# Joining the small product stages of an interleaved decoder block into common bursts, with a fourth weight buffer

## The chip, the core and the metric

The kernel runs on one core of a Trainium2 chip. The metric is the device time of one execution in microseconds (us); lower is better. A core has a matrix engine (TensorE, PE in the profile, with its weight loads shown as PEld), three engines for elementwise work (VectorE is DVE, ScalarE is ACT, GpSimd is POOL), and queues that issue DMA transfers (SP's is the one used for weights here).

## The reference

One decoder block on 256 tokens plus 16 meta tokens, all in float32 with a model width of 2048:

```
xn = rms(h)
z_rwkv, z_fox, z_gate = split(xn @ w_in)
y_a = rwkv7(token_shift(z_rwkv))          # 16 heads of 64: a linear recurrence over the tokens
y_b = fox(z_fox)                          # 16 heads of 64: causal attention with a forget gate
g_a, g_b = split(sigmoid(z_gate))
h = h + (g_a * (y_a @ w_a) + g_b * (y_b @ w_b)) @ w_o
gate, up = split(rms(h) @ w_gate_up)
out = h + (silu(gate) * up) @ w_down      # the 16 meta rows are dropped
```

The weights are 274 MB in all and are read once. Each float32 product is made of products of a high and a low part ("hl" in names), so that the matrix engine runs at its full rate.

## The kernel before

**The stream.** All weight products form one long stream of jobs on the matrix engine. A job takes one weight tile: `wload` (lines 301 to 325) issues the DMA into a `raw` tile (512 KB), ACT makes its high part `wh` (line 322) and DVE its low part `wl` (line 323). `raw` has `RAWB` buffers, `wh` and `wl` have `WB` buffers each, 3 of each here. `run` loads one job ahead of the one that multiplies. The order of instructions on the matrix engine is written out by hand (`manual_schedule`); the order on ACT, DVE, POOL and SP is made by the framework's scheduler, except for the first jobs.

**The order of the jobs.** First the `lora` jobs, then for each of four head groups g the projections k, v, r (272, 272 and 258 columns), a small job for decay and gate (`rwkv_w2` and so on), the FoX projections q, k, v (256, 272, 272 columns), and two gate jobs (256 columns). After the fourth group nine more gate jobs follow, then one more, then the branches, `w_o`, gate and up, and `w_down`.

**The small products.** Between the stream's matrix products stand the small ones of RWKV and FoX. Each of these chains is a Python generator that yields the planner's distance in ns until its next stage. `streams` holds the generators with their due times; `clock[0]` is the planner's clock, which counts only the stream's products. `slot` (line 360) is called after each triple of stream products (3n/2.4 ns of planner time for n columns). If a stage is due, the one with the earliest due time is emitted: its matrix products go into PE's order at this place, its other work to the other engines. After that, no stage comes for `GAP`, or for `MIX` times the stage's estimated matrix time `clock[2]`. I call the run of small matrix products of one stage a burst. The stages of one group with matrix products, in order:

- RWKV: `ss` and `kx` (norms of k), `mat` three times (the chunk matrices), `bs` (bonus), `trbk` twice, `trv`, `tr` (transposes); then a triangular solve on DVE with DMAs through DRAM (lines 829 to 849) and the wait `LANE`; then the chain: `rhs` of the meta tokens, `QT` with `u`, `X` with `s`, and four times `rhs`, `u` with `y`, `s` with `y`; last `yT`.
- FoX: `fss` twice and `fx` (norms), `pvm` with `pv` (transposes of v), and for each of two head pairs `sc` (scores, then softmax on DVE and ACT), `ppt` with `ptm` (transposes of the probabilities, copied to `pT` and `pM` by ACT), and `po` (the output).

These are 36 bursts a group, 144 in all, and one more of the forget gate. `psa` has four PSUM banks for them (`aux_ps`), the stream's own are in `psm`.

Of the kernel before, what the change touches and what calls it, by code (L numbers as in the profile page):

```python
# [12 lines left out]
AF = mybir.ActivationFunctionType  # L13
# [5 lines left out]
P = 128  # L19
D = 2048  # L20
NMETA = 16

T = 256
L = NMETA + T
# [23 lines left out]

RAWB = 3
WB = 3  # L50
ZB = 6
# [11 lines left out]
LANE = 24000  # L63
GAP = 250
LERP = 2800
BIAS = 7000
STEP = 1000
NORM = 4200
SUMS = 2000
X_RS = 1400  # L70
X_SPREAD = 1400
X_V = 1900
X_SC = 1600
X_EXP = 1100
X_DIV = 2600
X_PT = 1400
Y_SQ = 1400
# [6 lines left out]
Y_BONUS = 1200  # L84
Y_TRBK = 1400
Y_TRV = 1100
Y_TR0 = 1600
Y_RHS = 1400
Y_U = 1400
Y_XT = 1400  # L90
Y_QT = 1200
Y_GN = 1400
# [5 lines left out]
def hybrid_block(ctx, tc, A, out, dbg=None):  # L98
# [244 lines left out]

    def spawn(gen, delay):
        streams.append([clock[0] + delay, gen])

    def stage(st):
        try:
            st[0] = clock[0] + (next(st[1]) or HOP)
        except StopIteration:  # L350
            streams.remove(st)

    def pe_mm(out_, lhsT, rhs, start, stop, skip=False):
# [7 lines left out]
    def slot(ns):  # L361


        clock[0] += ns
        if clock[0] < clock[1]:
            return
        due = [st for st in streams if st[0] <= clock[0]]
        if due:
            clock[2] = 0.0
            stage(min(due, key=lambda st: st[0]))  # L370
            clock[1] = clock[0] + max(GAP, MIX * clock[2])

# [297 lines left out]
    def rwkv_bg(g, box):  # L670
# [15 lines left out]
        nc.scalar.activation(sq, kk, AF.Square)  # L686
        yield Y_SQ
        kn_ = rw.tile([P, 12], F32, tag="kn", name=f"kn{g}", bufs=2)
# [4 lines left out]
        backs = [spread(kr_, m, L, f"kx{g}{m}") for m in range(2)]  # L693
        yield Y_SPREAD
        for m in range(2):
# [37 lines left out]
        split(*parts, sq[:, :, :T])  # L733
        yield Y_AB

# [3 lines left out]
        for m in range(2):  # L739
            pss = [aux_ps(f"mat{g}{m}{h}") for h in range(2)]  # L740
            for c in range(4):
                for h in range(2):
                    pe_mm(pss[h][:, c * P:(c + 1) * P], bk[hb(h), m, c].rearrange("p x t -> p (x t)"),
                                     ar[hb(h), :, m, tok(c)], start=True, stop=True)
            for h in range(2):
                nc.vector.tensor_tensor(NK[:, h, 4 * m:4 * m + 4, :], pss[h].rearrange("p (c w) -> p c w", w=P),
                                        bcast(mup, 4), op=ALU.mult)
            yield Y_MAT
        pss = [aux_ps(f"mat0{g}{h}") for h in range(2)]
# [28 lines left out]
        for h in range(2):  # L778
            for m in range(2):
                nc.gpsimd.tensor_copy(NK[0:HD, h, 4 * m:4 * m + 4, 0:HD],  # L780
                                      ar[hb(h), 0, m, NMETA:].rearrange("p (c t) -> p c t", t=HD))
        yield Y_NEXT

        bo = ot(f"bo{g}")
        for m in range(2):
# [5 lines left out]
            nc.gpsimd.tensor_scalar(bo[:, m, :], bo[:, m, :], vi("gn_b", m), None, op0=ALU.add)  # L791
        yield Y_BONUS

# [5 lines left out]
        for m in range(2):  # L799
            ps = aux_ps(f"trbk{g}{m}")  # L800
            for c in range(4):
                pe_tr(ps[:, c * P:(c + 1) * P], bkf[:, 4 * m + c, :], ident)
            nc.scalar.activation(BK[:, :, 4 * m:4 * m + 4, :].rearrange("p h c d -> p c h d"),
                                 ps.rearrange("p (c h d) -> p c h d", h=2, d=HD), AF.Copy)
            yield Y_TRBK
        ps = aux_ps(f"trv{g}")
# [4 lines left out]
        for cc in range(2):  # L811
            nc.scalar.activation(SV[HD:, :, cc::2, :].rearrange("p h i d -> p i h d"),
                                 ps[hb(cc), :].rearrange("p (i h d) -> p i h d", h=2, d=HD), AF.Copy)
        yield Y_TRV
        ps = aux_ps(f"tr0{g}")
# [29 lines left out]
        for h in range(2):  # L845
            for q in range(2):
                nc.sync.dma_start(X[h * HD + 32 * q:h * HD + 32 * q + 32, :, 32 * q:32 * q + 32], d2v[h, q, :32])
            nc.sync.dma_start(X0[h * HD:h * HD + 16, :, 0:32], d3.rearrange("(h m) r t -> h r m t", h=2)[h])
        yield LANE

# [3 lines left out]
        def step(c, S, BK, SV, NK, X, Y):  # L854
# [11 lines left out]
            nc.scalar.activation(R, pv2(ps), AF.Copy)  # L866
            yield Y_RHS
            ps = aux_ps(f"u{g}{c}")
# [10 lines left out]
            for h in range(2):  # L879
                nc.vector.tensor_copy(SV[0:nt, h, mine, :], pv2(ps)[h * HD:h * HD + nt])  # L880
            yield Y_U
            if not last:
# [20 lines left out]
            if not first:  # L903
                nc.scalar.activation(Y.rearrange("p (m c) v -> p m c v", m=2)[:, :, c, :], pv2(psy), AF.Copy)
            yield HOP

# [7 lines left out]
        next(meta_steps)  # L914
        yield Y_XT
        ps = aux_ps(f"QT{g}")
# [6 lines left out]
        next(meta_steps)  # L923
        yield Y_QT
        ps = aux_ps(f"X12{g}")
# [22 lines left out]
        nc.vector.tensor_tensor(Y, Y, s2.unsqueeze(2).to_broadcast([P, 8, HD]), op=ALU.mult)  # L948
        yield NORM
        ps = aux_ps(f"yT{g}")  # L950
# [28 lines left out]
    def fox_jobs(g):  # L979
# [18 lines left out]
        def norms():  # L998
            while len(done) < 2:
                yield  # L1000
            yield from rsqrt_steps(fx, hr, hs, [P, 20], "ht")
            yield X_RS

            nc.vector.tensor_tensor(hs[:, 0:8], hs[:, 0:8], hr[:, 0:8], op=ALU.mult)
            backs = [spread(hr[:, 8:20], m, L, f"fx{g}{m}") for m in range(2)]
            yield X_SPREAD
            for m in range(2):
                nc.vector.tensor_tensor(kn[:, m, :], kn[:, m, :], backs[m](), op=ALU.mult)
            yield
            ready.append(1)  # L1010

        def post(dst, n):
            def f(pss):
                sqs = []
                for m in range(2):
                    ps = pss[m]
                    if dst is vv:
                        nc.scalar.activation(dst[:, m, :], ps[:, :n], AF.Copy)
                        continue
                    sq = fx.tile([P, L], F32, tag="sqf", name=f"sqf{g}", bufs=3)  # L1020
                    if dst is qn:
                        halves(dst[:, m, :], ps)
                        nc.scalar.activation(sq[:, :n], dst[:, m, :], AF.Square)
                    else:
                        nc.scalar.activation(sq[:, :n], ps[:, :n], AF.Square)
                        nc.scalar.activation(dst[:, m, :], ps[:, :n], AF.Copy, scale=qk8)
                    sqs.append(sq)
                if dst is vv:
                    spawn(fox_bg(g, qn, kn, vv, hs, hr, ready), HOP)
                else:  # L1030
                    spawn(sums(sqs, dst, n), SUMS)
                    if dst is kn:
                        spawn(norms(), PREP)
            return f
# [4 lines left out]
    def fox_bg(g, qn, kn, vv, hs, hr, ready):  # L1039
# [18 lines left out]
        cmb = cmask.unsqueeze(1).to_broadcast([P, 2, P])  # L1058
        for m in range(2):

# [9 lines left out]
            nc.gpsimd.tensor_tensor(bias[:, :, d1], bias[:, :, d1], cmb, op=ALU.add)  # L1070
            yield BIAS
            sums = fx.tile([P, 4], F32, tag="sums", name=f"sums{g}{m}", bufs=2)

            nq = [NMETA + P, L]
            cq_ = [slice(0, nq[0]), slice(nq[0], nq[0] + nq[1])]
# [5 lines left out]
            for t in range(2):  # L1081
                n = nq[t]
                for h in range(2):
# [7 lines left out]
                    nc.scalar.activation(s[:, :n], s[:, :n], AF.Exp, scale=r, bias=nm,  # L1091
                                         accum_out=sums[:, 2 * t + h:2 * t + h + 1])
            yield X_SC + X_EXP
            nc.vector.reciprocal(sums, sums)
            for t in range(2):
                for h in range(2):
                    s = sc_t[h, t][:, :nq[t]]
                    nc.vector.tensor_scalar(s, s, sums[:, 2 * t + h:2 * t + h + 1], None, op0=ALU.mult)
            yield X_DIV


            ptm = aux_ps(f"ptm{g}{m}")
            pts = []
            for h in range(2):
                ppt = aux_ps(f"ppt{g}{m}{h}")
                for c, t, k in ((T - 96, 0, 1), (0, 0, 0), (P, 1, 0), (T + 32, 1, 1)):
                    pe_tr(ppt[:, c:c + P], sc_t[h, t][:, k * P:(k + 1) * P], ident)
                pe_tr(ptm[:NMETA, h * P:(h + 1) * P], sc_t[h, 1][:, 2 * P:L], ident)
                pT = fx.tile([P, 416], F32, tag="pT", name=f"pT{g}{m}{h}", bufs=2)
                nc.scalar.activation(pT, ppt[:, :416], AF.Copy)  # L1110
                pts.append(pT)
            nc.scalar.activation(pM[:NMETA], ptm[:NMETA, :2 * P].rearrange("p (h q) -> p h q", h=2)[:, :, 96:], AF.Copy)
            yield X_PT
            po = aux_ps(f"po{g}{m}")
            for i in range(3):
                for h in range(2):
                    vs = slice(m * P + h * HD, m * P + (h + 1) * HD)
                    o = po[hb(h), :T]
                    if i == 0:
                        pe_mm(o, vt[:, 0, vs], pts[h][:, 0:T], start=True, stop=False)  # L1120
                    elif i == 1:
                        pe_mm(o[:, 96:], vt[:, 1, vs], pts[h][:, T:], start=False, stop=False)
                    else:
                        pe_mm(o[:, T - 32:], vm[:, vs], pM[:, h, :], start=False, stop=True)
            nc.scalar.activation(yb[:, 2 * g + m, :], po[:, :T], AF.Copy)
            yield

# [263 lines left out]
```

## Time and profile before

| what | value |
|---|---|
| median of three runs | 1565.6 us (1564.53, 1565.60, 1565.76) |
| the profiled execution: its own time, its span | 1564.75 us, 1563.0 us |
| busy: PE, PEld, DVE, ACT, POOL | 1553.5, 1366.3, 1015.7, 766.8, 104.3 us |
| granted TensorE clock, mean | 1.000 |
| read from HBM | 274.43 MB, 180 GB/s over the span |

The span runs from the first to the last instruction; the execution's own time has 1.75 us around it. Ends of matrix products are modelled, so what a burst costs is read from starts: how far apart two products of the stream stand with the burst between them, less what they are apart without one.

### The profile page before, as it was taken

What the parts mean: (1) busy time and instruction counts of PE and PEld (TensorE: products, weight loads), DVE (VectorE), ACT (ScalarE), POOL (GpSimd) and SP (SyncE); (2) the same over time, 40 slices, a digit from 0 to 9 for tenths busy, and PEclk for the clock granted to TensorE, in tenths of its full rate; (3) what the DMA queues carried; (4) which work ended last, traced back from release to release, by engine and by line L of the source; (5) the groups of instructions that cost most, each with busy time, mean ns of one, the idle gap of its engine ahead of it and who ended that gap; (6) DMA issues with size and microseconds to landing.
All of it is one profiled execution on the core that took longest, in us unless ns stands there. A gap on an engine that the chain in (4) does not pass through costs nothing.

```text
span 1563.0 us, 26173 instructions
## 1 busy us (share of the span) xinstructions
PE 1553.5 (99%) x10225; PEld 1366.3 (87%) x10225; DVE 1015.7 (65%) x1854; ACT 766.8 (49%) x1118; POOL 104.3 (7%) x194
## 2 busy tenths in 40 slices
PE   9999999999999999999999999999999999999998
PEld 9999988989889888999888888888888888888887
DVE  7878688677768856875655666566566656444443
ACT  6655455465445544654445554454445544333332
POOL 2121103102203100000000000000000000000000
PEclk9999999999999999999999999999999999999999
DMA  7556546546545566777666666666666666666664
GB/s 243 173 154 173 158 126 179 157 119 168 166 135 148 161 182 192 248 225 227 189 182 179 188 186 190 188 188 189 188 189 189 185 193 187 188 202 199 187 200 131
DMA packets 211483, 283.33 MB, mean 181 GB/s; under 512 B 23888, under 2 KB 128352, under 8 KB 211360
## 3 DMA queue, kind: packets, MB, share of 16 engines
q1 hardware_dynamic: 206752, 277.53, 60.8%
q10 hardware_dynamic: 4608, 4.13, 0.8%
q8 instruction: 80, 1.31, 0.4%
q14 instruction: 43, 0.35, 0.1%
HBM read 274.43 MB, written 7.19 MB: 180 GB/s over the span
## 4 chain that ended last, share of the span: by engine, by line
PE 94%; DVE 3%; DMA 1%; ACT 1%; issue 1%; SPq 0%; POOL 0%; DVEq 0%; ACTq 0%
PE up L392 10%; PE gt L392 10%; PE zg L392 7%; PE dn L1255 5%; PE dn L1253 5%; PE dn L1254 5%; PE up L394 5%; PE gt L394 5%; PE zg L394 3%; PE f L333 2%; PE f L392 2%; PE f L335 2%; PE f L334 2%; PE br L334 2%; PE br L335 2%; PE br L333 2%
## 5 line engine op out<-in xcount | busy, mean ns | idle before, releaser
L323 DVE TENSOR_TENSOR wl<-raw,wh 128x1024 fp32r<-128x1024 f32 (+1 forms) x496 | 605.3, 1221 | 439.7 <-ACT wh L322 437.8
L322 ACT ACTIVATE wh<-raw 128x1024 fp32r<-128x1024 f32 (+1 forms) x496 | 521.2, 1052 | 624.5 <-PE dn L1254 144.4
L392 PE MATMUL gt<-hts,wh 128*128 128x512 f32 x704 | 245.0, 394 | 0.0
L392 PE MATMUL up<-hts,wh 128*128 128x512 f32 x704 | 244.9, 394 | 0.0
L394 PE MATMUL gt<-hts,wl 128*128 128x256 f32 x660 | 186.2, 282 | 0.0
L394 PE MATMUL up<-hts,wl 128*128 128x256 f32 x660 | 186.0, 282 | 0.0
L392 PE MATMUL zg<-xhl,wh 128*128 128x512 f32 x512 | 184.3, 403 | 0.0
L392 PEld LDWEIGHTS up<-hts,wh 128*128 128x128 f32 x704 | 130.1, 188 | 26.4
L392 PEld LDWEIGHTS gt<-hts,wh 128*128 128x128 f32 x704 | 130.1, 188 | 26.3
L1254 PE MATMUL dn<-wh,acl 128*128 128x512 f32 x352 | 139.5, 396 | 0.0
L1253 PE MATMUL dn<-wh,ach 128*128 128x512 f32 x352 | 139.5, 396 | 0.0
L1255 PE MATMUL dn<-wl,ach 128*128 128x512 f32 x352 | 139.5, 396 | 0.0
L394 PE MATMUL zg<-xhl,wl 128*128 128x256 f32 x480 | 135.0, 281 | 0.0
L394 PEld LDWEIGHTS up<-hts,wl 128*128 128x128 f32 x660 | 124.7, 189 | 1.8
L394 PEld LDWEIGHTS gt<-hts,wl 128*128 128x128 f32 x660 | 124.7, 189 | 1.8
L392 PEld LDWEIGHTS zg<-xhl,wh 128*128 128x128 f32 x512 | 94.5, 188 | 20.8 <-issue 1.8
L394 PEld LDWEIGHTS zg<-xhl,wl 128*128 128x128 f32 x480 | 90.6, 189 | 1.1
L1255 PEld LDWEIGHTS dn<-wl,ach 128*128 128x128 f32 x352 | 66.3, 188 | 16.2
L1254 PEld LDWEIGHTS dn<-wh,acl 128*128 128x128 f32 x352 | 66.3, 188 | 16.2
L1253 PEld LDWEIGHTS dn<-wh,ach 128*128 128x128 f32 x352 | 66.3, 188 | 16.1
L333 PE MATMUL f<-xhl,wh 128*128 128x272 f32 x256 | 77.7, 303 | 0.0
L335 PE MATMUL f<-xhl,wl 128*128 128x272 f32 x256 | 73.8, 288 | 0.0
(459 smaller groups left out, 2777.6 us busy)
## 6 DMA issues: line engine op xcount, KB each, us to landing
raw<-in_w_gate_up_dram SPq DMA_DIRECT2D x176, 512.0 KB, 3.6
raw<-in_w_in_dram SPq DMA_DIRECT2D x160, 512.0 KB, 4.2
raw<-in_w_down_dram SPq DMA_DIRECT2D x88, 512.0 KB, 4.7
raw<-in_w_o_dram SPq DMA_DIRECT2D x32, 512.0 KB, 4.6
raw<-in_w_branch_a_dram SPq DMA_DIRECT2D x16, 512.0 KB, 3.9
raw<-in_w_branch_b_dram SPq DMA_DIRECT2D x16, 512.0 KB, 3.8
zgd<-zg ACTq DMA_DIRECT2D x30, 128.0 KB, 2.4
gate<-zgd SPq DMA_DIRECT2D x15, 256.0 KB, 5.8
```

The source lines that it names most:

```text
L322: nc.scalar.activation(wh[:prow, cs_], raw[:prow, cs_], AF.Copy)
L323: nc.vector.tensor_tensor(wl[:prow, cs_], raw[:prow, cs_], wh[:prow, cs_].bitcast(F32), op=ALU.subtract)
L333: nc.tensor.matmul(ps, wh, ah, start=first, stop=False)
L334: nc.tensor.matmul(ps, wh, al, start=False, stop=False)
L335: nc.tensor.matmul(ps, wl, ah, start=False, stop=last)
L392: nc.tensor.matmul(ps.rearrange("p (a t) -> p a t", a=2), wh, act, start=first, stop=last)
L394: nc.tensor.matmul(ps[:, :T], wl, act[:, 0, :], start=False, stop=False)
L1253: nc.tensor.matmul(box[t], ah[:, kt, ts_], wh[:, k, :], start=first, stop=False)
L1254: nc.tensor.matmul(box[t], al[:, kt, ts_], wh[:, k, :], start=False, stop=False)
L1255: nc.tensor.matmul(box[t], ah[:, kt, ts_], wl[:, k, :], start=False, stop=last)
```

## The change

- A stream now carries the number of PSUM banks that its next stage needs (0: a stage without matrix products). `slot` emits a due stage without products alone, as before. Of the due stages with products it emits all together that fit into four banks, in order of their due times. If only one is due, it is held for up to `HOLD` (2000 ns of planner time) when another one that fits comes due within that time.
- `trbk` of both halves become one stage, and `trv` with `tr` another. The scores of the second head pair (`sc`) are emitted in the stage of the first pair's `po`. `ptm` goes into the unused end of the `ppt` bank, with two copies to `pM` in place of one.
- `BIAS`, the wait of FoX ahead of its first scores, goes from 7000 to 28000 and stands once in place of twice; the second pair's biases are made in the softmax stage of the first. Other distances: `X_SPREAD` 1400 to 2400, `X_PT` 1400 to 2200 (4400 for the first pair), `Y_TRBK` 1400 to 2600, `Y_RHS`, `Y_U`, `Y_XT` 1400 to 1600, `Y_QT` 1200 to 2200.
- `RAWB` and `WB` go from 3 to 4. `dynamic_dma_scratch_size` is set to 2048 bytes, which frees SBUF for the buffers.

```diff
-RAWB = 3
-WB = 3
+RAWB = 4
+WB = 4
...
+HOLD = 2000
...
-    def spawn(gen, delay):
-        streams.append([clock[0] + delay, gen])
+    def spawn(gen, delay, banks=0):
+        streams.append([clock[0] + delay, gen, banks])
...
         clock[0] += ns
         if clock[0] < clock[1]:
             return
-        due = [st for st in streams if st[0] <= clock[0]]
-        if due:
+        due = sorted((st for st in streams if st[0] <= clock[0]), key=lambda st: st[0])
+        group = [st for st in due if not st[2]][:1]
+        if due and not group:
+
+            banks = 0
+            for st in due:
+                if banks + st[2] <= 8 - PSM:
+                    group.append(st)
+                    banks += st[2]
+            if (len(group) == 1 and clock[0] < due[0][0] + HOLD and
+                    any(st[2] and st[0] > clock[0] and st[0] < due[0][0] + HOLD and banks + st[2] <= 8 - PSM
+                        for st in streams)):
+                return
+        if group:
             clock[2] = 0.0
-            stage(min(due, key=lambda st: st[0]))
+            for st in group:
+                stage(st)
             clock[1] = clock[0] + max(GAP, MIX * clock[2])
...
-            yield Y_TRBK
+        yield Y_TRBK, 2
         ps = aux_ps(f"trv{g}")
...
-        yield Y_TRV
         ps = aux_ps(f"tr0{g}")
...
+        bs = biases(0)
+        yield BIAS, 2
+        sums = scores(0, *bs)
+        for m in range(2):
             yield X_SC + X_EXP
...
+            if m == 0:
+                bs = biases(1)
+            yield X_DIV, 2
...
                 ppt = aux_ps(f"ppt{g}{m}{h}")
+                pe_tr(ppt[:NMETA, 3 * P:], sc_t[h, 1][:, 2 * P:L], ident)
...
-                pe_tr(ptm[:NMETA, h * P:(h + 1) * P], sc_t[h, 1][:, 2 * P:L], ident)
...
+                nc.scalar.activation(pM[:NMETA, h, :], ppt[:NMETA, 480:], AF.Copy)
...
-            yield X_PT
+            yield (X_PT, 1) if m else (X_PT0, 3)
             po = aux_ps(f"po{g}{m}")
...
+            if m == 0:
+
+                sums = scores(1, *bs)
             nc.scalar.activation(yb[:, 2 * g + m, :], po[:, :T], AF.Copy)
-            yield
...
-    nc = _bacc.Bacc("TRN2", target_bir_lowering=False, num_devices=1)
+
+    nc = _bacc.Bacc("TRN2", target_bir_lowering=False, num_devices=1, dynamic_dma_scratch_size=2048)
```

## Rows read from the trace of the kernel before

**Rows 1.** The page, busy time by engine (us, share of the span, instructions)

```profile
PE 1553.5 (99%) x10225; PEld 1366.3 (87%) x10225; DVE 1015.7 (65%) x1854; ACT 766.8 (49%) x1118; POOL 104.3 (7%) x194
```

**Rows 2.** Windows view: stretch, length, busy us (instructions) by engine, clock, DMA share, GB/s

```profile
core 0: us, PE busy (x) PEld busy (x) DVE busy (x) ACT busy (x) POOL busy (x), PEclk, DMA share, GB/s
5.00:10.00 5.00, 4.89 (x34) 4.64 (x34) 4.41 (x9) 4.10 (x9) 4.64 (x20) 1.00 1.00 387
...
610.00:790.00 180.00, 180.00 (x1185) 164.32 (x1184) 123.67 (x156) 92.16 (x110) 0.00 (x0) 1.00 0.71 219
```

**Rows 3.** Waits view, PE alone, whole span: us in total, times, longest us

```profile
PE po L355 <- ACT pT L1110: 1.7, 1, 1.7
...
PE v L333 <- DVE fl L541: 0.8, 1, 0.8
PE f L392 <- ACT sig L655: 0.7, 1, 0.7
PE ppt L359 <- DVE s L1098: 0.6, 2, 0.3
```

**Rows 4.** Timeline of PE round a `rhs` burst: start us, us, engine, line, operation

```profile
424.15 0.29 PE L335 MATMUL v<-xhl,wl 128*128 128x272 f32 x1
424.37 0.45 PE L355 MATMUL rhs2-1_5581<-SV,NK 128*64 128x64 f32 x8
...
424.98 0.29 PE L334 MATMUL v<-xhl,wh 128*128 128x272 f32 x1
425.11 0.29 PE L335 MATMUL v<-xhl,wl 128*128 128x272 f32 x1
```

**Rows 5.** The same round a burst of `s` with `y`

```profile
439.52 0.28 PE L335 MATMUL r<-xhl,wl 128*128 128x258 f32 x1
439.74 0.45 PE L355 MATMUL s<-sv,bt 128*64 128x64 f32 x8
440.02 0.40 PE L355 MATMUL y<-sv,NK 128*64 128x64 f32 x8
...
440.57 0.28 PE L334 MATMUL r<-xhl,wh 128*128 128x258 f32 x1
```

**Rows 6.** The same round a burst of four transposes

```profile
240.55 0.29 PE L335 MATMUL f<-xhl,wl 128*128 128x272 f32 x1
240.67 0.60 PE L359 MATMUL trbk<-ident,bk 128*128 128x128 f32 x4
...
241.24 0.28 PE L334 MATMUL f<-xhl,wh 128*128 128x272 f32 x1
```

**Rows 7.** The same behind a burst of `fss`

```profile
101.98 1.13 PE L355 MATMUL fss<-bsum,sqf 128*128 128x2 f32 x12
103.04 0.39 PE L333 MATMUL f<-xhl,wh 128*128 128x272 f32 x1
103.27 0.29 PE L334 MATMUL f<-xhl,wh 128*128 128x272 f32 x1
```

**Rows 8.** Timeline of the stream, PE with its weight load

```profile
99.84 0.29 PE L334 MATMUL f<-xhl,wh 128*128 128x272 f32 x1
99.85 0.19 PEld L335 LDWEIGHTS f<-xhl,wl 128*128 128x128 f32 x1
```

**Rows 9.** Timeline of SP's queue between 395 and 425 us

```profile
406.59 1.91 SPq L841 DMA_DIRECT2D d<-lx  x3
408.55 3.00 SPq L843 DMA_DIRECT2D d<-lx  x4
411.74 2.24 SPq L847 DMA_DIRECT2D X<-d  x3
...
415.48 1.52 SPq L318 DMA_DIRECT2D raw<-in_w_in_dram  x3
```

**Rows 10.** Timeline of ACT in the same stretch

```profile
420.19 1.06 ACT L322 ACTIVATE wh<-raw 128x1024 fp32r<-128x1024 f32 x1 [5.22 <-DMA raw<-in_w_in_dram]
421.15 0.91 ACT L1110 ACTIVATE pT<-ppt 128x416 f32<-128x416 f32 x2
```

**Rows 11.** The page, costliest groups: busy us, mean ns, idle before

```profile
L322 ACT ACTIVATE wh<-raw 128x1024 fp32r<-128x1024 f32 (+1 forms) x496 | 521.2, 1052 | 624.5 <-PE dn L1254 144.4
```

**Rows 12.** The page, DMA queues: packets, MB, share

```profile
q1 hardware_dynamic: 206752, 277.53, 60.8%
q10 hardware_dynamic: 4608, 4.13, 0.8%
q8 instruction: 80, 1.31, 0.4%
```

More of the change, by code (lines that the diff above doesn't have):

```diff
@@ L64 @@
 GAP = 250
+HOLD = 2000
 LERP = 2800
-BIAS = 7000
+BIAS = 28000
 STEP = 1000
@@ L70 @@
 X_RS = 1400
-X_SPREAD = 1400
+X_SPREAD = 2400
 X_V = 1900
@@ L75 @@
 X_DIV = 2600
-X_PT = 1400
+X_PT = 2200
+X_PT0 = 4400
 Y_SQ = 1400
@@ L84 @@
 Y_BONUS = 1200
-Y_TRBK = 1400
-Y_TRV = 1100
+Y_TRBK = 2600
 Y_TR0 = 1600
[L88 to L91, printed above, removed]
+Y_RHS = 1600
+Y_U = 1600
+Y_XT = 1600
+Y_QT = 2200
 Y_GN = 1400
@@ L342, in hybrid_block @@
     clock = [0.0, 0.0, 0.0]
-    def spawn(gen, delay):
-        streams.append([clock[0] + delay, gen])
+    def spawn(gen, delay, banks=0):
+        streams.append([clock[0] + delay, gen, banks])
     def stage(st):
         try:
-            st[0] = clock[0] + (next(st[1]) or HOP)
+            step = next(st[1]) or HOP
         except StopIteration:
             streams.remove(st)
+            return
+        step, st[2] = step if isinstance(step, tuple) else (step, 0)
+        st[0] = clock[0] + step
     def pe_mm(out_, lhsT, rhs, start, stop, skip=False):
@@ L366, in slot @@
             return
-        due = [st for st in streams if st[0] <= clock[0]]
-        if due:
+        due = sorted((st for st in streams if st[0] <= clock[0]), key=lambda st: st[0])
[9 more added lines that the diff above has]
+                        for st in streams)):
+                return
+        if group:
             clock[2] = 0.0
-            stage(min(due, key=lambda st: st[0]))
+            for st in group:
+                stage(st)
             clock[1] = clock[0] + max(GAP, MIX * clock[2])
@@ L686, in rwkv_bg @@
         nc.scalar.activation(sq, kk, AF.Square)
-        yield Y_SQ
+        yield Y_SQ, 1
         kn_ = rw.tile([P, 12], F32, tag="kn", name=f"kn{g}", bufs=2)
@@ L693, in rwkv_bg @@
         backs = [spread(kr_, m, L, f"kx{g}{m}") for m in range(2)]
-        yield Y_SPREAD
+        yield Y_SPREAD, 2
         for m in range(2):
@@ L733, in rwkv_bg @@
         split(*parts, sq[:, :, :T])
-        yield Y_AB
+        yield Y_AB, 2
         NK = nkt(f"NK{g}")
@@ L747, in rwkv_bg @@
                                         bcast(mup, 4), op=ALU.mult)
-            yield Y_MAT
+            yield Y_MAT, 2
         pss = [aux_ps(f"mat0{g}{h}") for h in range(2)]
@@ L781, in rwkv_bg @@
                                       ar[hb(h), 0, m, NMETA:].rearrange("p (c t) -> p c t", t=HD))
-        yield Y_NEXT
+        yield Y_NEXT, 2
         bo = ot(f"bo{g}")
@@ L791, in rwkv_bg @@
             nc.gpsimd.tensor_scalar(bo[:, m, :], bo[:, m, :], vi("gn_b", m), None, op0=ALU.add)
-        yield Y_BONUS
+        yield Y_BONUS, 2
         BK, SV = (bst(t, f"{t}{g}") for t in ("bt", "sv"))
@@ L848, in rwkv_bg @@
             nc.sync.dma_start(X0[h * HD:h * HD + 16, :, 0:32], d3.rearrange("(h m) r t -> h r m t", h=2)[h])
-        yield LANE
+        yield LANE, 1
         pv2 = lambda ps: ps[:, :2 * HD].rearrange("p (m v) -> p m v", v=HD)
@@ L866, in step @@
             nc.scalar.activation(R, pv2(ps), AF.Copy)
-            yield Y_RHS
+            yield Y_RHS, 2
             ps = aux_ps(f"u{g}{c}")
@@ L880, in step @@
                 nc.vector.tensor_copy(SV[0:nt, h, mine, :], pv2(ps)[h * HD:h * HD + nt])
-            yield Y_U
+            yield Y_U, 2
             if not last:
@@ L904, in step @@
                 nc.scalar.activation(Y.rearrange("p (m c) v -> p m c v", m=2)[:, :, c, :], pv2(psy), AF.Copy)
-            yield HOP
+            yield (HOP, 0) if last else (HOP, 1)
         S = [None]
@@ L914, in rwkv_bg @@
         next(meta_steps)
-        yield Y_XT
+        yield Y_XT, 2
         ps = aux_ps(f"QT{g}")
@@ L923, in rwkv_bg @@
         next(meta_steps)
-        yield Y_QT
+        yield Y_QT, 2
         ps = aux_ps(f"X12{g}")
@@ L948, in rwkv_bg @@
         nc.vector.tensor_tensor(Y, Y, s2.unsqueeze(2).to_broadcast([P, 8, HD]), op=ALU.mult)
-        yield NORM
+        yield NORM, 1
         ps = aux_ps(f"yT{g}")
@@ L1005, in norms @@
             backs = [spread(hr[:, 8:20], m, L, f"fx{g}{m}") for m in range(2)]
-            yield X_SPREAD
+            yield X_SPREAD, 2
             for m in range(2):
@@ L1028, in f @@
                 if dst is vv:
-                    spawn(fox_bg(g, qn, kn, vv, hs, hr, ready), HOP)
+                    spawn(fox_bg(g, qn, kn, vv, hs, hr, ready), HOP, 2)
                 else:
-                    spawn(sums(sqs, dst, n), SUMS)
+                    spawn(sums(sqs, dst, n), SUMS, 1)
                     if dst is kn:
@@ L1058, in fox_bg, with biases @@
         cmb = cmask.unsqueeze(1).to_broadcast([P, 2, P])
-        for m in range(2):
+        def biases(m):
             bias = fx.tile([P, 2, L], F32, tag="bias", name=f"bias{g}{m}", bufs=1)
@@ L1070, in fox_bg, with scores @@
             nc.gpsimd.tensor_tensor(bias[:, :, d1], bias[:, :, d1], cmb, op=ALU.add)
-            yield BIAS
+            return b1, bias
+        nq = [NMETA + P, L]
+        def scores(m, b1, bias):
             sums = fx.tile([P, 4], F32, tag="sums", name=f"sums{g}{m}", bufs=2)
-            nq = [NMETA + P, L]
             cq_ = [slice(0, nq[0]), slice(nq[0], nq[0] + nq[1])]
@@ L1092, in fox_bg @@
                                          accum_out=sums[:, 2 * t + h:2 * t + h + 1])
+            return sums
+        bs = biases(0)
+        yield BIAS, 2
+        sums = scores(0, *bs)
+        for m in range(2):
             yield X_SC + X_EXP
@@ L1098, in fox_bg @@
                     nc.vector.tensor_scalar(s, s, sums[:, 2 * t + h:2 * t + h + 1], None, op0=ALU.mult)
-            yield X_DIV
-            ptm = aux_ps(f"ptm{g}{m}")
+            if m == 0:
+                bs = biases(1)
+            yield X_DIV, 2
             pts = []
@@ L1105, in fox_bg @@
                 ppt = aux_ps(f"ppt{g}{m}{h}")
+                pe_tr(ppt[:NMETA, 3 * P:], sc_t[h, 1][:, 2 * P:L], ident)
                 for c, t, k in ((T - 96, 0, 1), (0, 0, 0), (P, 1, 0), (T + 32, 1, 1)):
                     pe_tr(ppt[:, c:c + P], sc_t[h, t][:, k * P:(k + 1) * P], ident)
-                pe_tr(ptm[:NMETA, h * P:(h + 1) * P], sc_t[h, 1][:, 2 * P:L], ident)
                 pT = fx.tile([P, 416], F32, tag="pT", name=f"pT{g}{m}{h}", bufs=2)
                 nc.scalar.activation(pT, ppt[:, :416], AF.Copy)
+                nc.scalar.activation(pM[:NMETA, h, :], ppt[:NMETA, 480:], AF.Copy)
                 pts.append(pT)
-            nc.scalar.activation(pM[:NMETA], ptm[:NMETA, :2 * P].rearrange("p (h q) -> p h q", h=2)[:, :, 96:], AF.Copy)
-            yield X_PT
+            yield (X_PT, 1) if m else (X_PT0, 3)
             po = aux_ps(f"po{g}{m}")
```

## The prediction

> **What bounds the kernel now.** I read the page first: PE is busy 99% of the span, DVE and ACT far less [rows 1]. Busy time alone proves little, because matrix products overlap, so I looked at the stream's starts: products of 272 columns start 0.13 us apart [rows 4], and each weight load runs beside the product before it [rows 8]. After the small products, from 610 to 790 us, PE has no gap at all [rows 2]. So the time is PE's order of instructions, one behind the other. It can get shorter in two ways: PE waits less, or what stands in its order costs less. The waits view is the measure for the first: 1.7 + 0.8 + 0.7 + 0.6 = 3.8 us are all the waits of note in the whole span [rows 3]. For the second I took single bursts apart in PE's timeline.
>
> **What a burst costs beyond its products.** From the start of L335 ahead of the `rhs` burst to the start of L334 behind it are 424.98 − 424.15 = 0.83 us; without a burst two steps of 0.125 would be 0.25, so eight products cost 0.58 [rows 4]. Sixteen of the same shape (`s` with `y`) cost 440.57 − 439.52 − 0.24 = 0.81 [rows 5]. So eight more cost 0.23, and a burst as such costs 0.58 − 0.23 = 0.35 us: the way into and out of products that use a part of the array (128*64). Two such bursts joined save 0.35 us. Four transposes cost 241.24 − 240.55 − 0.25 = 0.44 us, 0.11 each [rows 6]; their fixed part I take as nothing, as the stretch holds nothing but four even steps. `fss`, `ss` and `kx` lie between: behind `fss` the next step of the stream is 0.23 us in place of 0.125 [rows 7], so 0.10 us is what I can see of a fixed part; 0.35 is the upper bound.
>
> **What is joined.** I wrote down the due times of the stages with the constants of the diff, each stage at the first free slot. This tells nothing of the chip's time, only which stages stand together. Between the second and third groups' starts the pattern settles; for group 1's head and group 0's chain it reads, in planner us: `sc` 99; `ppt`+`rhs` 105; `QT`,`u` 107; `X`,`s` 109; `po`+`sc` 110; `rhs` 112; `u`+`ppt` 116; `s`+`po` 118; `rhs`+`ss` 122; `u` 124; `s` 125; `kx`+`rhs` 129; `fss`+`u` 130; `s` 132; `rhs` 135; `u`+`mat` 138; `s`+`fss` 140; `mat` 142; `mat` 145; `bs` 147; both `trbk`+`fx` 150; `yT`+`v` 152; `trv`+`tr` 152.5. Over four groups 145 bursts become 96. The 49 joins by kind:
> - Both parts pay a full fixed cost: `po`+`sc` 4 times (written into the code, so certain), `s`+`po` 4, `u`+`mat` 3. 11 × 0.35 = 3.85 us.
> - One part is `ss`, `kx` or `fss`: 4 kinds in three groups and 2 in the first, 14 × 0.10 = 1.4 us (4.9 at the upper bound).
> - The other 24 have transposes or `bs` in them (all of the merged `trbk`, `trv` and `tr` among them): nothing, by the price above.
>
> **The waits that are there.** The 1.7 us wait of `po` for `pT` [rows 3]: behind the solve SP issues the transfers to `d` and `X` from 406.59 to 415.3 us, and the next raw loads come only at 415.48 [rows 9]. The conversion `wh` then waits 5.22 us for its data, and ACT, which works in order, makes `pT` behind it [rows 10]. A fourth buffer holds one more job, some 3 us of stream (24 steps of 0.125), ahead of this jam; I take the full 1.7 off. Two waits of `ppt` for `s`, 0.6 in all: `X_DIV` is as before, but the stage moves from the gate jobs, where DVE has more to do, into v and r jobs for three groups; I take half, 0.3, bounds 0 and 0.6. The waits of 0.8 and 0.7 near 45 and 71 us are for DVE and ACT, which also convert weights there; a fourth buffer lets some conversions run earlier. I take 0.5, bounds −0.5 and 1.5: earlier raw loads also meet the stretch where DMA is full (share 1.00 [rows 2]). In all 2.5 us.
>
> **What costs nothing.** The scratch for dynamic DMA: all transfers listed run on queues of the hardware and on those that load instructions [rows 12], none of the software's. Two copies to `pM` in place of one, and the earlier biases on POOL: ACT is 49% and POOL 7% busy [rows 1], and the biases of the second pair still have X_DIV + X_PT0 = 7000, what BIAS gave them. The bias transfers go into SP's queue 20 us earlier, with one more raw load of cover. The fourth buffers behind 610 us: no PE gap is left there to fill. `yT` of the last group comes 4 us of planner time later, 8 us ahead of the end of the nine gate jobs, so the branches do not wait for it; without this cover they would wait those 4 us.
>
> **New waits.** A joined burst takes up to four PSUM banks at once, all there are. The planner counts a group's own banks, not those that ACT and DVE still have to empty. Three places are tight: `po`+`sc` (three banks) 1.3 planner us behind `X`,`s` in three groups and 0.6 in the last; `QT`,`u` 1.7 behind `ppt`+`rhs`; `trv`+`tr` 0.6 behind `yT`+`v` in three groups. 11 places. Below: nothing, since no bank is waited for in the trace now [rows 3]. Above: one weight conversion on ACT in front of the emptying copy, 1.05 us [rows 11], 11.6 in all. I take 0.2 a place, 2.2 us, nearer to the lower end because bank waits are absent now with stages as close as 1 us.
>
> **Sum.** 3.85 + 1.4 + 2.5 − 2.2 = 5.55 us less. The profiled execution took 1564.75 us, so 1559.2; the median is 0.85 above it, so I forecast 1560 us for the median.
>
> **Rivals.** 0.2%, 3.1 us, is about what a measurement can tell from no change.
> 1. *Every join pays.* If transposes too paid 0.35 on their way in and out, 49 × 0.35 = 17.2 us, with the waits 17.2 + 2.5 − 2.2 = 17.5 less: 1548. Against it: four transposes cost four even steps [rows 6], and the stream's own loads run hidden over the full array [rows 8]. By the Trainium skill, "TensorE: Matmul & The Clock Gate", in Part 3, "The mechanism" (what overlaps and what doesn't), a weight load overlaps running products only when it goes to another row group; by that rule alone a burst over all rows would pay like a narrow one. The trace disagrees: the load at 99.85 us runs beside the product at 99.84, both over 128 rows, which fits the background weight buffer that the same section also names. Chance 5%.
> 2. *The joins cost what they save* (no change). Either the joins outside the code miss each other, leaving 1.4 + 2.5 − 2.2 = 1.7 us: 1564; or the bank waits are 0.5 us a place, 5.5 in all: 1563.3. For it: the stages wait for slots, so my due times may be off by 1 to 2 us, though HOLD mends just that. Chance 20%.
> 3. *Banks become the bound* (slower). Joined bursts of three or four banks stand at some 7 places in each group. If each must wait for the copies of the burst before it, behind one conversion of 1.05 us [rows 11], that is 28 × 1.05 = 29 us, less 7.8 of gains: 1587; from 11/28 = 0.4 us a place it is slower than now by more than 0.2%. Against it: ACT and DVE have 51% and 35% of the span free [rows 1], and the longer distances. Chance 12%.
>
> The forecast has 63%: its own range is 1555 (14 joins at 0.2, all the waits gone, no new ones) to 1562.5. With rival 1 faster has 0.68, the same 0.20, slower 0.12. For 8 in 10 I leave out rival 1 and most of rival 3: 1553 (all 14 joins at 0.35, all the waits of 3.8 gone, no new one) to 1566.
>
> **What would show it.** PE's timeline should show some 96 bursts; `po` and `sc` back to back, together some 0.35 us cheaper than apart; transposes at 0.11 each wherever they stand. The wait of `po` for `pT` should be gone, with raw loads issued before SP's jam. The waits view of PE should list bank waits (for ACT's copies of `X`, `pT`, `vt`) of 2 us in all. I am wrong if those are over 6 us, if transposes got cheaper by joining, or if PE waits for raw data again.

## The result and the profile after

The changed kernel takes 1569.59 us (median of 10 runs, 1568.35 to 1570.72) against 1565.49 us for the kernel before: ratio 1.0026, 95% interval 1.0018 to 1.0034. It is 4.1 us slower, where I had forecast 5.5 us faster and a range that ends at 1566. The busy times of the page, which answer to [rows 1], hardly move:

```profile
PE 1549.0 (99%) x10225; PEld 1365.6 (87%) x10225; DVE 1014.2 (65%) x1854; ACT 764.8 (49%) x1126; POOL 95.1 (6%) x194
```

The waits of PE over the whole span do move. This view answers to [rows 3]:

```profile
PE mat L360 <- DVE bk L738: 3.9, 3, 3.4
PE pv L364 <- ACT ya L976: 2.6, 1, 2.6
PE fx L364 <- ACT ya L976: 1.6, 2, 0.9
PE s0-1_2320 L360 <- DVE SV L897: 1.2, 1, 1.2
...
PE v L335 <- DVE fl L559: 0.9, 1, 0.9
PE yT L364 <- ACT bt L821: 0.6, 1, 0.6
PE trv L364 <- DVE kn L1025: 0.6, 1, 0.6
```

The old waits of `po` for `pT`, of `ppt` for `s` and of the one near 71 us are gone. In their place stand 10.5 us of waits in the joined bursts or just around them (all rows but that of `v`). They are of three kinds: for a late product of DVE (`mat`), for a bank that is not yet empty (`pv`, `fx`, `yT`, `trv`) and for a copy that DVE makes late (`s0-1`). The joins as such do what they should. PE's timeline round a burst of `s` with `y` and `po`:

```profile
191.42 0.28 PE L412 MATMUL f<-xhl,wl 128*128 128x256 f32 x1
191.63 0.45 PE L360 MATMUL s<-sv,bt 128*64 128x64 f32 x8
191.91 0.40 PE L360 MATMUL y<-sv,NK 128*64 128x64 f32 x8
192.15 0.88 PE L360 MATMUL po<-pT,vt 128*64 128x256 f32 x8
192.85 0.26 PE L360 MATMUL po<-pM,vm 128*64 128x32 f32 x4
193.04 0.50 PE L410 MATMUL f<-xhl,wh 128*128 128x512 f32 x1
193.38 0.28 PE L412 MATMUL f<-xhl,wl 128*128 128x256 f32 x1
```

From 191.42 to 193.38 are 1.96 us, 0.35 of them the stream's own two steps (0.12 + 0.23), so the burst costs 1.61. Apart, `s` with `y` costs 0.81 [rows 5] and a `po` 1.14 in the kernel before (median of its eight): 0.34 saved. Now the same view where the chain's last `u` with `y` and the next group's `mat` share a burst:

```profile
221.97 0.29 PE L337 MATMUL f<-xhl,wl 128*128 128x272 f32 x1
222.18 0.45 PE L360 MATMUL u<-R,X 64*64 64x64 f32 x8
222.46 0.40 PE L360 MATMUL y<-S,ar 64*64 64x64 f32 x8
226.30 1.59 PE L360 MATMUL mat<-ar,bk 64*128 64x128 f32 x16 [3.44 <-DVE bk L738]
227.82 0.59 PE L335 MATMUL f<-xhl,wh 128*128 128x272 f32 x1
228.22 0.43 PE L336 MATMUL f<-xhl,wh 128*128 128x272 f32 x1
228.44 0.43 PE L337 MATMUL f<-xhl,wl 128*128 128x272 f32 x1
```

PE stands idle for 3.44 us, and behind it the stream's steps are 0.22 us apart in place of 0.125. The windows view shows why (clock in the third column from the end):

```profile
222.00:227.00 5.00, 1.56 (x30) 1.30 (x30) 3.94 (x9) 0.25 (x1) 0.00 (x0) 0.99 0.37 105
226.80:230.30 3.50, 3.50 (x23) 3.27 (x21) 1.22 (x2) 2.20 (x4) 0.00 (x0) 0.51 0.00 0
```

Behind the idle stretch PE was granted half its clock, 1.2 GHz, for 3.4 us. From `mat` at 226.30 to the product of L336 at 230.26 are 3.96 us; the same products take some 2.45 where the clock is full (1.09 from `mat` to L335 as in after_ar2 below, 0.23 to L336, and nine steps of 0.125), so the half clock loses some 1.5 us more, an estimate. What DVE did meanwhile:

```profile
222.68 0.61 DVE L897 COPY sv<-u 64x128 f32<-64x128 f32 x2 [0.81 <-PE u L360]
223.21 0.71 DVE L729 SCALAR_TENSOR_TENSOR ar<-k,sig 128x544 f32<-128x544 f32 x1
...
225.47 0.68 DVE L738 TENSOR_TENSOR bk<-k,cs 128x512 f32<-128x512 f32 x1
226.07 0.18 DVE L739 TENSOR_TENSOR bk<-k,cs 128x32 f32<-128x32 f32 x1
```

It first waits for `u`, then makes `ar` and `bk`, on which `mat` depends. So `mat` waits for work that starts only behind the first half of its own burst.

The longest bank wait is that of `pv`, joined with the chain's `yT`:

```profile
253.24 1.23 DVE L325 TENSOR_TENSOR wl<-raw,wh 128x1024 fp32r<-128x1024 f32 x1 [3.52 <-ACT wh L324]
254.50 0.86 DVE L978 COPY ya<-yT 64x256 f32<-64x256 f32 x2
255.39 0.38 ACT L976 ACTIVATE ya<-yT 64x256 f32<-64x256 f32 x1 [1.91 <-DVE ya L978]
255.82 0.44 PE L364 MATMUL pv<-ident,vv 128*128 128x128 f32 x2 [2.64 <-ACT ya L976]
```

`pv` does not read `ya`, so what it waits for is taken to be the bank of `yT`; `fx`, `yT` and `trv` are read in the same way. DVE empties its part of that bank only behind a weight conversion, and ACT the last part behind DVE.

The wait of `s0-1` for `SV` begins on POOL. The change has it make the second pair's biases here, ahead of the `zd` that DVE needs first, and DVE then makes the copy `SV` behind both:

```profile
166.55 0.90 POOL L1085 TENSOR_SCALAR b<-bias,cq,hs 128x144 f32<-128x144 f32 x2 [5.94 <-DMA bias<-ncd]
...
169.90 0.65 POOL L463 TENSOR_TENSOR zd<-z 128x272 f32<-128x272 f32 x1
170.58 0.50 DVE L466 SCALAR_TENSOR_TENSOR v<-zd,vcol,z 128x272 f32<-128x272 f32 x1 [5.54 <-POOL z L454]
172.68 0.59 DVE L897 COPY SV<-u0-1_2273 16x128 f32<-16x128 f32 x2
```

**The balance.** I took all bursts by the starts around them, as in [rows 4], and set each against its parts' medians in the kernel before. Before: 145 bursts, 125.0 us, of which 3.6 are waits. After: 91 bursts, 128.8 us; the bursts without a wait save 4.6 us by being joined, the nine with one cost 11.9 us more than their parts: 6.2 at banks, 4.1 at `mat`, 1.6 at `s0-1`. −4.6 + 11.9 − 3.6 = 3.7 us. The two profiled executions differ by 3.6 us (1568.35 − 1564.75), the medians by 4.1. (The expectations below reckon with 12.2 for the 11.9.) Outside the bursts stand about 1 us of the half clock and, the other way, the wait of 0.7 near 71 us that is gone.

### The profile page after: what moved, and what is told of

Its sections match the earlier page's. It is cut to its first block, busy times and chain, and to the rows that moved or that the text cites. A ratio compares the mean times of both kernels' runs of the same rounds, so it can differ in the third digit from the quotient of the medians.

```text
span 1566.6 us, 26165 instructions
## 1 busy us (share of the span) xinstructions
PE 1549.0 (99%) x10225; PEld 1365.6 (87%) x10225; DVE 1014.2 (65%) x1854; ACT 764.8 (49%) x1126; POOL 95.1 (6%) x194
## 4 chain that ended last, share of the span: by engine, by line
PE 82%; DVE 1%; ACT 0%; issue 0%; ACTq 0%
PE up L410 10%; PE gt L410 10%; PE zg L410 7%; PE dn L1286 5%; PE dn L1285 5%; PE dn L1284 5%; PE up L412 5%; PE gt L412 5%; PE zg L412 3%; PE br L336 2%; PE br L337 2%; PE br L335 2%; PE wo L1285 2%; PE wo L1286 2%; PE wo L1284 2%; PE f L335 1%
## 5 line engine op out<-in xcount | busy, mean ns | idle before, releaser
L335 PE MATMUL f<-xhl,wh 128*128 128x272 f32 x256 | 77.1, 301 | 0.0
```

The source lines that it names most:

```text
L335: nc.tensor.matmul(ps, wh, ah, start=first, stop=False)
```

## The experiments

Theory A was that stages in one burst wait for each other's banks and inputs; B that FoX beside the chain costs the time; C that the buffers do. E and F came later. The runs were taken in four sets, each on a chip of its own and with its own runs of the kernel before (medians 1563.4, 1564.28, 1563.81 and 1564.89), so ratios are compared. The changed kernel itself gave 1.0026 at first and 1.0036 in a later set (after_again), so a difference of a thousandth between sets tells little.

**no_join** is the changed kernel with the joining taken out of `slot`:

```diff
-        due = sorted((st for st in streams if st[0] <= clock[0]), key=lambda st: st[0])
-        group = [st for st in due if not st[2]][:1]
...
+        due = [st for st in streams if st[0] <= clock[0]]
+        group = [min(due, key=lambda st: st[0])] if due else []
```

> The changed kernel, but one due stage at a time and no hold; all else (distances, FoX beside the chain, merged transposes, four buffers) stays. Theory A (the loss is waits of PE inside or right behind joined bursts, 12.2 us in the changed kernel's trace; the joins themselves save 4.6): the joins' 3.8 us outside the code's own po+sc are lost, and about 10 us of waits go: about 1563.5 us, 1561 to 1566. Rival B (the loss comes from FoX beside the chain or from the other distances, whatever is joined): 1569 or more, as the joins' saving is lost and nothing is gained.

1560.05 us, ratio 0.9979 (0.9970 to 0.9988). So all else in the change together gains, though no more than its buffers do alone (next run); the joining and holding cost some 7.4 us against it. B falls.

**buffers_alone** is the kernel before with four buffers:

```diff
-RAWB = 3
-WB = 3
+RAWB = 4
+WB = 4
```

> The kernel before with four raw, wh and wl buffers and the small scratch, nothing else. Theory A: the buffers cost nothing and take away the wait of po for pT (2.1 us by starts) and perhaps part of the 1.5 us of early waits: 1562 to 1565. Rival C (the buffers or their other places in SBUF cost the time): 1567 or more.

1560.83 us, ratio 0.9983 (0.9974 to 0.9992): 2.6 us faster. Its waits of PE:

```profile
PE warmup L296 <- DVE yb L293: 1.1, 1, 1.1
PE v L333 <- DVE fl L541: 0.8, 1, 0.8
```

`po`, `ppt` and the wait near 71 us are gone, 3.0 us of idle time.

**three_buffers** is the changed kernel with 3 again:

> The changed kernel with three buffers as before. Theory A: up to 2 us slower than the changed kernel, as a raw load behind the solve's transfers can again be late: 1569.6 to 1572. Rival C: faster than the changed kernel by 2 us or more.

1570.74 us, ratio 1.0046 (1.0032 to 1.0059), above the changed kernel's 1.0026 and 1.0036 by 1 to 2 thousandths. C, which needs it faster, falls. That the fourth buffers gain is clear in the kernel before alone; here the intervals overlap.

**transposes_alone** takes the banks off the stages of transposes, so that they are emitted alone, as in

```diff
-        yield Y_SPREAD, 2
+        yield Y_SPREAD
```

> The changed kernel, but the stages of transposes (kx, fx, trbk, trv with tr, yT, pv, ppt) are emitted alone, when due, as before; the other joins stay. Theory A: the bank waits of fx, trv, pv, yT (6.2 us by starts) go, the wait of mat for bk (4.2) and of s for sv (1.6) stay, and some 0.7 us of savings are lost: about 1564, 1562.5 to 1566.5. Rival D (the banks are short because the transposes were merged and moved closer, joined or not): within 1.5 us of the changed kernel, 1568 to 1570. Rival B: the same as D.

1566.42 us, ratio 1.0018 (1.0008 to 1.0027), not clear of the changed kernel's 1.0026: by the ratios as small a gain as D forecast, and smaller than A's. The waits of `fx`, `pv`, `yT`, `trv` and of `mat` went, but new ones came:

```profile
PE y L360 <- DVE sv L897: 4.9, 3, 1.7
PE trbk L364 <- ACT bt L821: 2.1, 3, 0.7
```

and three stretches of 3.4 us at half clock. Here `mat` stands alone, and the chain's last step waits: one half of its `sv` copy lies on DVE behind the block that makes `ar` and `bk`:

```profile
216.33 0.28 DVE L897 COPY sv<-u 64x128 f32<-64x128 f32 x1
...
220.05 0.29 DVE L897 COPY sv<-u 64x128 f32<-64x128 f32 x1
```

This spoke against A: the trouble follows two streams that meet, not one burst. Theory E: holding makes the chain late, and its end falls on the next group's DVE block. In the kernel before, the chain's last `u` starts at 215.34 us and `mat` at 224.25, 8.9 us apart; in no_join 213.63 and 222.53; in the changed kernel they share a burst.

**no_join_late** tests it without any join: no_join with `LANE` 28500 in place of 24000.

> The kernel of no_join (no joins, no hold) with LANE 28500 in place of 24000, so that the chain's last steps come as late as the holds make them in the changed kernel, on top of the next group's DVE block that makes ar and bk for mat. Theory E (the time is lost because the chain slips into that DVE block, joined or not): waits of PE for bk or sv of 1.5 to 3.5 us in up to three groups, some with the half clock behind them: 5 to 10 us slower than no_join, ratio to before 1.001 to 1.004. Rival A (the waits come from two stages standing in one burst): within 1.5 us of no_join, ratio 0.997 to 0.999.

1574.47 us, ratio 1.0067 (1.0054 to 1.0080): 14 us slower than no_join by the ratios, slower than every joined kernel, and beyond the 1.004 at which E's range ended. PE's waits:

```profile
PE mat L360 <- DVE bk L727: 4.8, 2, 2.4
PE fx L364 <- ACT ya L965: 2.9, 2, 1.5
PE y L360 <- DVE sv L886: 1.7, 1, 1.7
```

A falls as a rule for the large waits: they come with no burst joined. The wait of `fx` for `ya`, a bank wait, is among them.

**hold0** is the changed kernel with `HOLD = 0`.

> The changed kernel with HOLD 0: stages are joined when both are due, none is held back. By the due times few joins are left but po+sc, and the chain is not late. Theory E: about as no_join, ratio 0.996 to 0.999. Rival A: between the changed kernel and no_join by the number of joined bursts, which is small here too, but a wait wherever a joined burst of four banks is left, above all pv with trv and tr: ratio 0.999 to 1.001.

1558.35 us, ratio 0.9963 (0.9950 to 0.9975), 5.9 us faster than before and, with heads_alone (next), the fastest. From no_join, which joins nothing in `slot`, it is not clear of the noise. 126 bursts are left, with 2.1 us saved by joins and no wait in any:

```profile
PE v L335 <- DVE fl L559: 1.2, 1, 1.2
PE warmup L298 <- DVE yb L295: 1.1, 1, 1.1
```

**heads_alone** keeps the hold, but takes the banks off all stages at a group's head and off `yT`, by edits as in transposes_alone.

> The changed kernel, but the stages at the head of a group (ss, kx, fss, mat, bs, trbk, trv, fx, pv) and yT are emitted alone and hold nothing; only the chain and FoX's sc, ppt, po are joined. By the due times the chain then ends as early as before. Theory E: no wait for bk or sv, two joins a group of 0.2 to 0.35 us gained: 1 to 2.5 us faster than no_join, ratio 0.996 to 0.998. Rival A: waits at the joined bursts that are left, as fast as no_join or slower: 0.998 to 1.001.

1558.93 us, ratio 0.9965 (0.9952 to 0.9979). Joins save 3.5 us, the most without a late chain; three waits of `trbk` for `ya` (2.3 us idle, 3.0 by starts) take most of it back.

**heads_unmerged** and **heads_spaced** were meant to take that wait off, the first with `trbk`, `trv`, `tr` as four stages again, the second with `Y_BONUS` 2800 in place of 1200.

> heads_alone with trbk, trv and tr as four stages again, at the distances of before (1400, 1400, 1100). Theory E with the bank waits as a second part: the wait of trbk for ya in no_join (1.0 us idle, 1.4 by starts) goes: 0.5 to 1.5 us faster than heads_alone, the fastest version. Rival: the merge of the transposes gains by itself, then it is slower than heads_alone.

> heads_alone with Y_BONUS 2800 in place of 1200, so that trbk comes 1600 of planner time later behind yT. Theory E with its second part (trbk waited 2.3 us idle, 3.0 by starts, because ACT had not yet emptied yT's bank): that wait goes, 2 to 3 us faster than heads_alone, ratio 0.9945 to 0.9955 and the fastest version. Rival: fx, trbk and pv then stand closer together and wait for each other's banks instead: 0.996 or more.

1560.94 us, ratio 0.9979 (0.9970 to 0.9988), and 1561.25 us, 0.9982 (0.9973 to 0.9991): both slower than heads_alone by the medians (the intervals touch). The wait of `trbk` for `ya` went in both. But in each, the chain of one group slipped onto the DVE block again (`y` waits 2.0 us for `sv`, half clock behind it). The gain that theory E promised came in neither; each edit moved the chain as well as the stage it was meant for.

**after_again** is the changed kernel in the set of heads_spaced.

> The changed kernel once more, unchanged, so that it stands on the same chip and against the same runs of the kernel before as the next one: ratio 1.0018 to 1.0034 as in its first timing, with the same waits of mat for bk and of pv and fx for ya. If chips differ by more than that, its ratio leaves this interval.

1569.38 us, ratio 1.0036 (1.0023 to 1.0048), just outside the interval named, with the same waits; `s` waited 1.6 us for `SV` here and half clock followed there too.

**after_ar2** and **late_ar2** ask why a late chain makes PE wait. `ar` has one buffer; the chain reads it until its last `u` with `y`, so the next group's `ar` can't be written earlier (theory F). A second buffer needs room, so `raw` goes back to three:

```diff
-RAWB = 4
+RAWB = 3
...
-        ar = rw.tile([P, 2, 2, L], F32, tag="ar", name=f"ar{g}", bufs=1)
+        ar = rw.tile([P, 2, 2, L], F32, tag="ar", name=f"ar{g}", bufs=2)
```

> The changed kernel with two buffers for ar (and three for raw, to make room; wh and wl keep four). Theory F (the next group's ar has the one buffer that the chain reads until its last u with y, so its DVE block of 4.5 us can start only behind that burst, and mat, emitted in or right behind the same burst, waits for it): the waits of mat for bk (3.9 us idle) and the half clock behind them (some 1.7) go, the bank waits of pv, fx, trv stay: 4 to 6 us faster than the changed kernel, ratio to before 0.999 to 1.001. Theory E in its first form (only DVE's order and load matter, not the buffer): within 1.5 us of the changed kernel, 1.0025 to 1.0045.

> no_join_late (no joins, chain late) with two buffers for ar (three for raw). Theory F: the waits of mat for bk (4.8 us idle) and most of that of y for sv (1.7) go, with two or three of the stretches at half clock: 6 to 9 us faster than no_join_late, ratio 1.001 to 1.003, with the waits of fx for ya left. Theory E in its first form: as no_join_late, 1.0055 to 1.008.

after_ar2: 1566.56 us, ratio 1.0009 (1.0000 to 1.0018). late_ar2: 1568.85 us, 1.0023 (1.0012 to 1.0033), 4.4 thousandths below no_join_late. Both ratios are as F has them; in microseconds after_ar2 gains 2.7 on the changed kernel's first ratio and 4.2 on its second, where F had 4 to 6. The half clock is gone from after_ar2; in late_ar2 the two stretches behind `mat` are gone, and two others came, one of them behind a wait of `v` for `z` of 2.2 us. The wait of `mat` for `bk` is gone from both; the burst of `u`, `y`, `mat` in after_ar2:

```profile
227.02 0.45 PE L360 MATMUL u<-R,X 64*64 64x64 f32 x8
227.30 0.40 PE L360 MATMUL y<-S,ar 64*64 64x64 f32 x8
227.63 1.16 PE L360 MATMUL mat<-ar,bk 64*128 64x128 f32 x16
228.72 0.39 PE L335 MATMUL f<-xhl,wh 128*128 128x272 f32 x1
```

and DVE writes `ar` 7 to 9 us ahead of the chain's last read at 227.30:

```profile
218.72 0.68 DVE L741 TENSOR_TENSOR ar<-r,dd 128x512 f32<-128x512 f32 x1
...
219.96 0.71 DVE L729 SCALAR_TENSOR_TENSOR ar<-k,sig 128x544 f32<-128x544 f32 x1
```

What is left in after_ar2:

```profile
PE v L335 <- DVE z L455: 2.1, 1, 2.1
PE fx L364 <- ACT ya L976: 1.9, 2, 1.2
PE pv L364 <- ACT ya L976: 1.7, 1, 1.7
...
PE yT L364 <- ACT bt L821: 0.6, 1, 0.6
PE trv L364 <- DVE kn L1025: 0.6, 1, 0.6
```

The bank waits stay. The wait of `s0-1` is gone as well and others are new (`v` for `z` 2.1 us, `QT` 0.9, `sc` 0.5), so the ratio does not price the second buffer by itself; what it shows of the buffer is that `mat` no longer waits. That the wait of `v` comes from the raw buffer given up is not shown, since in three_buffers, which has three as well, it is 0.2 us.

**heads_ar2** is the control, heads_alone with the same edit:

> heads_alone with two buffers for ar (three for raw). There the chain is not late, so by theory F the second buffer gains nothing: 0.996 to 0.998, and the waits of trbk for ya stay. If DVE's order is freed by it all the same, under 0.996.

1561.54 us, ratio 0.9980 (0.9971 to 0.9989): no gain where the chain is not late. By the ratios 1.5 thousandths are lost, with a wait of `v` for `z` of 1.2 us near the start that heads_alone has not, but the intervals overlap.

## Why the prediction was wrong

- **The fixed price of a burst** was right in kind. Pairs of partial-array bursts saved 0.34 (`s`+`po`), 0.33 (`rhs`+`po`) and 0.20 us (`po`+`sc`, `u`+`po`) where I took 0.35; those with `ss`, `kx` or `fss` 0 to 0.2 where I took 0.10. (The longer step behind `fss`, from which I took the 0.10, stands behind transposes too, 241.03 to 241.24 [rows 6], where I took nothing; so it was no measure.) The joins gave 4.6 us against 5.25, in part by luck: 91 bursts came in place of 96, in other pairs than I listed, and `u` met `mat` once in place of three times.
- **Transposes** joined with each other saved nothing (`pv` with `trv` and `tr`: 1.53 to 1.54 us together, 1.55 apart), with a partial-array burst 0 (`ppt`+`rhs`) to 0.12. Rival 1, by which every join pays 0.35, is refuted.
- **The waits that were there**: right for `po`. 2.5 us predicted, 2.6 by buffers_alone, but that the sums agree is partly luck: I put the gain at `ppt` down to its new place, and the buffers alone took it, twice as large (0.6).
- **New waits**: here it failed, 2.2 us predicted and 11.9 measured. The step "The planner counts a group's own banks, not those that ACT and DVE still have to empty" named one cause and missed two others. The bank waits proper (`pv`, `fx`, `yT`, `trv`) are 5.4 us of idle time, 6.2 by starts, at the transposes around `yT`, of which I named one place; the places behind `X`,`s` and behind `ppt`+`rhs` made no bank wait. My argument from a trace without bank waits did not carry over: there the end of one group's chain and the head of the next stood apart, and it is mostly where they meet that PE waits. The largest single wait (3.4 us) has nothing to do with PSUM: `u`+`mat`, which I booked as three gains of 0.35, join two streams that share one buffer of `ar`.
- **What costs nothing**: one item did cost. I set the earlier biases on POOL at nothing because POOL is 7% busy, but POOL did them ahead of `zd`, for which DVE, and behind it `SV` and `s0-1`, waited: 1.6 us by starts. This is read from two traces (the changed kernel, after_again); no run takes it off alone.
- **HOLD**: I called it a mend for due times that miss each other. It holds the chain until it meets the next group, and that lateness costs more than the joins give: HOLD 0 alone turns 1.0026 into 0.9963, though it keeps less than half of the joins' savings; all three kinds of new waits are gone from its trace.
- **Half clock** was not in the sum: some 1.5 us behind the wait of `mat`.
- **The signs of being wrong** did not cover this: transposes got no cheaper, PE did not wait for raw data, and the bank waits stayed under 6 us idle, though none was for the copies that I named (`X`, `pT`, `vt`).
- Rival 3 was right in its sign, and its banks are half of the story; after_ar2 leaves 1.0009 with those waits in it.
- Open: what the bank waits alone cost. heads_unmerged and heads_spaced moved the chain as well, so no run takes those waits off and nothing else. no_join_late, where `fx` waits 2.9 us for `ya` with nothing joined, shows that the late chain alone can bring them; by starts they are 5.6 us in after_ar2.

## What to carry to other kernels

Before joining or delaying stages of two pipelined chains, list each buffer that both use in turn (here one `ar`), and check that the delayed last reader still stands ahead of the next writer by the writer's whole block. Here a join gave at most 0.35 us, and the joins kept their gain where the chain did not come late (hold0: 2.1 us saved, no wait) and lost it twice over where it did (4.6 saved, 11.9 lost): holding a stage back moves everything behind it in its chain. A low busy share (POOL's 7%) does not say that work put in front of other work on that engine is free. And where PE was full, a wait of 1.4 to 3.4 us at times cost some 1.5 us again through the clock.

## What the runs showed of the hardware

The clock fell to half for 3.41 us behind some idle stretches of PE and not behind others. In transposes_alone it did behind each of the three waits of `y` (1.5 to 1.7 us); here is the first, with the clock third from the end:

```profile
217.00:220.90 3.90, 2.35 (x22) 2.00 (x21) 3.87 (x9) 1.71 (x3) 0.00 (x0) 1.00 0.00 0
220.96:224.30 3.34, 3.34 (x16) 3.34 (x16) 3.31 (x6) 0.98 (x3) 0.00 (x0) 0.50 0.49 147
```

In the changed kernel the wait of 2.6 us for `pv` and in the kernel before the 1.7 us for `po` had no such stretch. By the Trainium skill, "TensorE: Matmul & The Clock Gate", Part 1, "What's actually happening", the clock gate has a half state for an idle PE and a full state for a busy one. The granted 1.00 and 0.50 agree. Why the half state follows some waits and not others the rows don't tell.
